# A hybrid decoder layer whose down projection puts tokens, not model columns, on the output partitions

## The chip, the cores and the metric

The kernel runs on one core of a Trainium2 chip. The metric is the device time of one execution in microseconds (us), the median of several runs. Engines are named as in the profile: PE is TensorE's matmul, PEld its weight load, DVE is VectorE, ACT ScalarE, POOL GpSimd, SP the engine that issues most DMAs.

## The reference

One layer for 512 prompt tokens and for 32 sample tokens (8 sequences of 4 new tokens, each with a past of 4096 rows in a paged cache). All data are f32; model width 1024, feed-forward width 4096.

```
h   = x + W_out [ DiffAttn(4 heads) ; ChunkGatingMLP(512 channels) ](RMSNorm(x))
out = h + W_down relu(W_up RMSNorm(h))^2
```

The feed-forward part is the one that the change concerns:

```python
def sq_relu_ffn(h, g, w_up, w_down):
    return jnp.square(jax.nn.relu(rms_norm(h, g) @ w_up)) @ w_down
```

The row scale r of RMSNorm is left out of the activations in the kernel: relu(r z)^2 = r^2 relu(z)^2, so the down projection's result is multiplied by r^2, token by token, and then added to h.

## The kernel before, in words

**Precision.** A product in f32 is made of three matmuls on fp32r halves: high by high, high by low, low by high. Weights come as raw f32 pieces of 512 KB (four blocks of 128 rows by 256 columns); `w_conv` (line 262) splits a piece into `wh` (cast on ACT) and `wl` (subtraction on DVE); `w_get` (line 280) hands the pair to PE. `w_issue` (line 241) starts loads on SP in the order of the list `WL`, at most `RAWB` ahead.

**Stages.** Up to some 363 us: input projection, prompt attention, gating, output projection (`out_proj`, line 1051), with tokens on the output partitions; a matmul there has 128 tokens stationary and 256 weight columns moving. The residual rows h stand in `hN[t]`, token tile t on the partitions. `h_tr` (line 1126) transposes h into eight tiles `acc[m]`, model columns on the partitions; `h_split` (line 1133) writes the halves `Thi` and `Tlo`. Then come eight groups of 512 feed-forward channels (`ffn`, line 1140). The decode attention (`micro`) is fed in between by `pump` (line 691): each `yield` of the main work gives a cost, and steps of the attention are emitted in proportion. It ends in group 4.

**A group.** Up: for each of four blocks of 128 channels, 24 matmuls with weights stationary and tokens moving. `square` (nested in `ffn`) does relu on ACT, the square on DVE, the high half `ahi` on ACT and the low half `alo` on DVE. Down: four blocks of 256 model columns (`dp`), weights stationary, tokens moving, result in accumulator tiles with model columns on the partitions; DVE adds them to `acc[m]`. In the first three activation slices both halves of 128 columns are begun before the fourth slice is touched.

**Sample tokens.** In groups 0 to 4 moving columns are the 512 prompt tokens. The sample's h is ready only in group 4 (`out_sample`, line 1315). Groups 5 to 7 (joint) move 544 columns, in two matmuls of 272. The sample's share of groups 0 to 4 is made up for by `ffn_sample` (line 1248) inside groups 5 to 7, from unsplit f32 weights: `tiled` (line 1243) puts four products of 32 tokens side by side on the PE array, which leave four partial sums on the 128 partitions of `ysum`.

**Row scale and end.** The sum in `acc` starts as h divided by r^2: `spread` (line 1107) brings the factors of the tokens to all partitions with four products with `ones`, and multiplies `acc`. In the last group `sum_sample` (line 1273) joins the four partial sums, and `finish` (line 1223), put off by `later` until the next `flush` (line 295), transposes a block of columns back (two transposes for the sample, eight for the prompt), scales by r^2 and stores.

**Order.** Instructions are emitted in the order of the code, and a planner then fixes each engine's order from modelled times. `Ordered` (line 41) limits it: on PE and DVE an instruction may go at most 28 places ahead.

Of the kernel before, what the change touches and what calls it, by code (L numbers as in the profile page):

```python
# [30 lines left out]
NPL = 6  # L31
PLX = 2
WINDOW = 28
P_AT = 10
# [28 lines left out]
def kernel(  # L63
# [53 lines left out]
    def second_phase():  # L117
        local.close()
        phase1.close()
        pools["tw"] = T  # L120
        local_pool(8)
        pools["w"] = ctx.enter_context(tc.tile_pool(name="wp2", bufs=2))
        psd2 = ctx.enter_context(tc.tile_pool(name="psd2", bufs=3, space=bass.MemoryType.PSUM))
        pools["ps"] = [psd, psd2, psd, psd2, psd, psd2, psd, psd]
        st["plain"] = NPL
        while w_issue():
            pass
        for _ in range(2):
            w_conv()
# [32 lines left out]
    alo = []  # L162
    ysum = []
    idt = const.tile([128, 128], F32, name="idt")
    ones = const.tile([128, 128], F32, name="ones")
# [59 lines left out]

    def add(main, extra=(), rate=1):
        for n, pieces in enumerate(main):
            WL.extend((w, True) for w in pieces)
            WL.extend((w, False) for e in extra for x in e[rate * n:rate * n + rate] for w in x)

    add(wo_pieces())
    for g in range(NG):
        add(group_pieces(g), [wo_pieces()] if g == G1 - 1 else [group_pieces(j) for j in samples(g)] if g >= G1 else (),
            2 if g == NG - 1 else 1)

    raws = []
    plain = []
    cvt = []
    st = {"next": 0, "issued": 0, "done": 0, "plain": 0}

    def w_issue(t=None):

        if st["next"] == len(WL):
            return False
        src, split_it = WL[st["next"]]
        if split_it:
            if t is None:
                if st["issued"] >= st["done"] + RAWB:
                    return False
                t = wp.tile([128, 4, 256], F32, tag="raw", name="raw", bufs=RAWB)  # L250
            raws.append(t)
            st["issued"] += 1
        else:
            if len(plain) >= st["plain"]:
                return False
            t = pools["w"].tile([128, 4, 256], F32, tag="plain", name="plain", bufs=st["plain"] + PLX)
            plain.append(t)
        SP.dma_start(out=t, in_=src)
        st["next"] += 1
        return True  # L260

    def w_conv():

        i = st["done"]
        if raws:
# [8 lines left out]
            V.tensor_tensor(out=lo, in0=raw, in1=hi, op=ALU.subtract)  # L274
            cvt.append((hi, lo))
            st["done"] += 1
            while w_issue():
                pass

    def w_get():  # L280
        return cvt.pop(0)

# [8 lines left out]
    def later(fn, d=1):  # L291

        pend[d - 1].append(fn)
# [757 lines left out]
    def out_proj(att):  # L1051
        acc.extend(R[2 + m // 4][:, (m % 4) * T:(m % 4) * T + T] for m in range(8))
        ss = ssb[0]
        for p in range(4):
            A_, B_ = w_get(), w_get()
            cols = slice(256 * p, 256 * p + 256)
            for tp in range(2):
# [6 lines left out]
                if p == 3 and tp == 1:  # L1064
                    for m in range(6):
                        h_split(m, slice(0, 256), acc[m][:, 0:256])
                if p == 2 and tp == 0:
                    for t in (R[2], R[3]):
                        G.memset(t.rearrange("p (m t) -> p m t", m=4)[:, :, 512:544], 0.0)
                for half, w in W:  # L1070
# [33 lines left out]
        V.tensor_scalar(out=ms, in0=ms, scalar1=EPS, scalar2=None, op0=ALU.add)  # L1104
        V.tensor_copy(out=rst8, in_=ms)

        def spread():
            psr = dt_()
            for t in range(4):
                dg = zt_()[:, 0:128]  # L1110
                V.tensor_scalar(out=dg, in0=idt, scalar1=rst8[:, t:t + 1], scalar2=None, op0=ALU.mult)
                mm(psr[:, 128 * t:128 * t + 128], ones, dg, True, True)
            rb = tt_()
            A.copy(out=rb[:, 0:512], in_=psr)
            for m in range(8):
                V.tensor_tensor(out=acc[m][:, 0:512], in0=acc[m][:, 0:512], in1=rb[:, 0:512], op=ALU.mult)
            rsqrt(ms, 0.0)
            V.tensor_tensor(out=rst[:, 0:4], in0=ms, in1=ms, op=ALU.mult)
        later(spread)
        for i in range(2):  # L1120
            t = big.tile([128, 4 * T], F32R, tag=f"r{i}", name=f"a{i}")
            for o in (0, 2 * T):
                ahi.append(t[:, o:o + T])
                alo.append(t[:, o + T:o + 2 * T])
# [15 lines left out]
    def ffn(start, joint, last, small):  # L1140
        rng = [(0, 272), (272, 544)] if joint else [(0, 512)]
        n = T if joint else TP

        def step():
# [4 lines left out]
        def square(ps, ff):  # L1149
            r = tt_()  # L1150
            for q, (a, e) in enumerate(rng):
                A.activation(out=r[:, a:e], in_=ps[q][:, 0:e - a], func=ACTF.Relu)
            V.tensor_tensor(out=r[:, 0:n], in0=r[:, 0:n], in1=r[:, 0:n], op=ALU.mult)
            A.copy(out=ahi[ff][:, 0:n], in_=r[:, 0:n])
            V.tensor_tensor(out=alo[ff][:, 0:n], in0=r[:, 0:n], in1=ahi[ff][:, 0:n], op=ALU.subtract)

        for pr in range(2):
# [17 lines left out]
            for f in range(2):  # L1175
# [19 lines left out]
                yield 2.8  # L1195
            step()
        for dp in range(4):
            hiw, low = w_get()
            ps = [[dt_() for _ in rng] for _ in range(2)]
            for ffs in ((0, 1), (2, 3)) if last else ((0, 1, 2), (3,)):  # L1200
                if ffs[0]:
                    flush()
                for d in range(2):
                    dc = slice(128 * d, 128 * d + 128)
                    for ff in ffs:
                        for w, (st_w, mv) in enumerate(((hiw, ahi), (hiw, alo), (low, ahi))):
                            for q, (a, e) in enumerate(rng):
                                mm(ps[d][q][:, 0:e - a], st_w[:, ff, dc], mv[ff][:, a:e], ff == 0 and w == 0, ff == 3 and w == 2)
            w_conv()
            for d in range(2):  # L1210
                m = 2 * dp + d
                for q, (a, e) in enumerate(rng):
                    V.tensor_tensor(out=acc[m][:, a:e], in0=acc[m][:, a:e], in1=ps[d][q][:, 0:e - a], op=ALU.add)
            step()
            if last and dp == 0:
                later(sum_sample)
            yield 5.6
            if last:
                later(lambda dp=dp: finish(dp))
        if last:  # L1220
            flush()

    def finish(dp):

        cols = slice(256 * dp, 256 * dp + 256)
        ps = dt_()
        for d in range(2):
            PE.transpose(ps[0:32, 128 * d:128 * d + 128], acc[2 * dp + d][:, 512:544], idt)
        zs = zt_()
        V.scalar_tensor_tensor(out=zs[0:32], in0=ps[0:32, 0:256], scalar=rst[0:32, 4:5], in1=ysum[0][0:32, cols],  # L1230
                               op0=ALU.mult, op1=ALU.add)
        SP.dma_start(out=ys[:, cols], in_=zs[0:32])
        for tp in range(2):
            ps = dt_()
            for k in range(4):
                t, d = 2 * tp + k // 2, k % 2
                PE.transpose(ps[:, 128 * k:128 * k + 128], acc[2 * dp + d][:, 128 * t:128 * t + 128], idt)
            z = tt_()[:, 0:512]
            V.tensor_scalar(out=z[:, 0:256], in0=ps[:, 0:256], scalar1=rst[:, 2 * tp:2 * tp + 1], scalar2=None, op0=ALU.mult)
            A.activation(out=z[:, 256:512], in_=ps[:, 256:512], func=ACTF.Copy, scale=rst[:, 2 * tp + 1:2 * tp + 2])  # L1240
            SP.dma_start(out=yp[:, 2 * tp:2 * tp + 2, cols], in_=z.rearrange("p (t c) -> p t c", t=2))

# [5 lines left out]
    def ffn_sample():  # L1248
# [17 lines left out]
        for dp in range(4):  # L1266
# [4 lines left out]
            yield 0.5  # L1271

    def sum_sample():
        t = pools["w"].tile([32, 1024], F32, tag="xs", name="part", bufs=1)
        for b in range(1, 4):
            A.copy(out=t, in_=ysum[0][32 * b:32 * b + 32, :])
            V.tensor_tensor(out=ysum[0][0:32], in0=ysum[0][0:32], in1=t, op=ALU.add)
        V.tensor_scalar(out=ysum[0][0:32], in0=ysum[0][0:32], scalar1=rst[0:32, 4:5], scalar2=None, op0=ALU.mult)

# [35 lines left out]
    def out_sample():  # L1315
        stack.append(pools["w"].tile([128, 32], F32, tag="stack", name="stack", bufs=1))
        for b in range(4):
            V.tensor_copy(out=stack[0][32 * b:32 * b + 32], in_=idt[32 * b:32 * b + 32, 32 * b:32 * b + 32])
        xs = pools["w"].tile([32, 1024], F32, tag="xs", name="hs", bufs=1)
        SP.dma_start(out=xs, in_=xs_d)  # L1320
        for p in range(4):
# [21 lines left out]
        def go():  # L1343
# [11 lines left out]
            G.memset(y, 0.0)  # L1355
            V.tensor_scalar(out=y[0:32], in0=xs, scalar1=ss[:, 0:1], scalar2=None, op0=ALU.mult)
            rsqrt(ss[:, 0:1], 0.0)
            V.tensor_tensor(out=rst[0:32, 4:5], in0=ss[:, 0:1], in1=ss[:, 0:1], op=ALU.mult)
        later(go)
# [44 lines left out]
```

## Time and profile before

| | us |
|---|---|
| timed runs, median (lowest, highest) | 843.15 (841.08, 843.17) |
| profiled execution, its own time | 842.67 |
| its span | 841.0 |
| PE busy in the span | 812.3 (97%) |
| PEld, DVE, ACT, POOL busy | 630.6, 547.7, 357.9, 187.0 |

Busy is the time in which at least one instruction of the engine runs. Matmuls overlap one another, so that PE's share tells that it seldom stands still, and not how fast it goes; the distance between two starts tells that.

### The profile page before, as it was taken

The numbers are of one execution on the slowest core, as the hardware profiler recorded it, in microseconds if no ns is written. First come the engines' busy times: TensorE is split into PE (matmuls) and PEld (weight loads), VectorE is DVE, ScalarE is ACT, GpSimd is POOL, SyncE is SP. The second block draws the span as 40 slices with busy tenths as digits, with TensorE's granted clock in tenths as the row PEclk, the third lists the DMA queues.
The fourth block names the chain that finished last, engine by engine and source line by source line (L and its number), as shares of the span: only waits on it lengthen the run. The fifth ranks groups of instructions, "written<-read, shape, count | busy, mean of one in ns | idle before, by whom it ended". The sixth has DMA issues, their size and how long they took to land.

```text
span 841.0 us, 15425 instructions
## 1 busy us (share of the span) xinstructions
PE 812.3 (97%) x6210; PEld 630.6 (75%) x6210; DVE 547.7 (65%) x957; ACT 357.9 (43%) x888; POOL 187.0 (22%) x196
## 2 busy tenths in 40 slices
PE   5899999999899999999999999999999999999997
PEld 5788788676566788876666766655776898998997
DVE  5978766899888954787767576633844535444354
ACT  4543734776564652735144144163332431331231
POOL 4453532243432321212222232120100000000000
PEclk8899999999999999999999999999999999999999
DMA  8496799788788889877989797786398177577302
GB/s 316 156 376 227 264 356 317 298 317 328 279 312 322 296 307 334 291 244 281 321 316 344 294 346 275 281 294 230 116 317 267 61 237 245 177 234 232 101 14 94
DMA packets 101796, 219.06 MB, mean 260 GB/s; under 512 B 6088, under 2 KB 83996, under 8 KB 85340
## 3 DMA queue, kind: packets, MB, share of 16 engines
q0 software_dynamic: 18432, 134.23, 42.7%
q1 hardware_dynamic: 83292, 83.84, 30.5%
q8 instruction: 49, 0.80, 0.4%
q14 instruction: 23, 0.19, 0.1%
HBM read 213.53 MB, written 4.52 MB: 259 GB/s over the span
## 4 chain that ended last, share of the span: by engine, by line
PE 77%; DVE 8%; ACT 7%; DMA 5%; issue 2%; POOL 1%; SPq 0%; DVEq 0%; POOLq 0%; ACTq 0%
PE d L52 66%; PE O L52 6%; PE S L52 5%; DVE kt L52 3%; ACT PT L52 3%; DMA kraw<-in_cache_k_dram,idxK 2%; DMA raw<-in_w_in_dram 2%; DVE wl L52 1%; ACT wh L52 1%; DMA sg<-in_subln_gain_dram 1%; ACT z L52 1%; DVE s L52 1%; ACT t L52 1%; DVE zn L52 1%; ACT P L52 0%
## 5 line engine op out<-in xcount | busy, mean ns | idle before, releaser
L52 ACT CAST wh<-raw 128x1024 fp32r<-128x1024 f32 x90 | 94.1, 1047 | 189.2 <-PE d L52 175.4
L52 PE MATMUL d<-a,wh 128*128 128x272 f32 (+1 forms) x704 | 168.2, 342 | 0.4 <-DVE a L52 0.4
L52 DVE STREAM_TRANSPOSE kt<-kraw 128x2048 f32<-128x2048 f32 x64 | 146.8, 2300 | 13.5 <-PE S L52 7.1
L52 DVE TENSOR_TENSOR wl<-raw,wh 128x1024 fp32r<-128x1024 f32 x90 | 109.3, 1218 | 54.6 <-ACT wh L52 54.2
L52 PEld LDWEIGHTS d<-a,wh 128*128 128x128 f32 x704 | 112.8, 188 | 29.4 <-issue 7.1
L52 POOL DMA_INDIRECT v<-in_cache_v_dram,idxK x64 | 72.9, 1139 | 269.8 <-PE O L52 252.2
L52 PE MATMUL d<-wh,Thi 128*128 128x256 f32 x432 | 127.6, 296 | 0.6 <-ACT d L52 0.5
L52 PE MATMUL d<-wl,Thi 128*128 128x256 f32 x432 | 122.4, 283 | 0.0
L52 PE MATMUL d<-wh,Tlo 128*128 128x256 f32 x432 | 122.1, 283 | 0.2 <-DVE Tlo L52 0.2
L52 PE MATMUL d<-Thi,wh 128*128 128x272 f32 (+2 forms) x368 | 109.8, 339 | 0.0
L52 PE MATMUL d<-Tlo,wh 128*128 128x272 f32 (+2 forms) x368 | 106.7, 330 | 1.9 <-DVE Tlo L52 1.9
L52 PE MATMUL d<-Thi,wl 128*128 128x272 f32 (+2 forms) x368 | 106.8, 330 | 0.0
L52 PE MATMUL d<-a,wl 128*128 128x272 f32 (+1 forms) x352 | 102.7, 336 | 0.0
L52 PEld LDWEIGHTS d<-wh,Thi 128*128 128x128 f32 x432 | 81.6, 189 | 17.1 <-issue 11.5
L52 POOL DMA_INDIRECT kraw<-in_cache_k_dram,idxK x64 | 69.1, 1080 | 104.5 <-DVE kt L52 59.8
L52 PEld LDWEIGHTS d<-wh,Tlo 128*128 128x128 f32 x432 | 81.6, 189 | 0.9 <-issue 0.4
L52 PEld LDWEIGHTS d<-Thi,wh 128*128 128x128 f32 x368 | 63.7, 189 | 24.5 <-issue 15.0
L52 PEld LDWEIGHTS d<-wl,Thi 128*128 128x128 f32 x432 | 81.4, 188 | 0.0
L52 PE MATMUL O<-v,PT 128*32 128x512 f32 x512 | 73.4, 607 | 1.2 <-ACT PT L52 1.2
L52 ACT COPY PT<-d 32x128 f32<-32x128 f32 x256 | 65.6, 256 | 14.4 <-DVE d L52 11.0
L52 PEld LDWEIGHTS d<-Tlo,wh 128*128 128x128 f32 x368 | 63.9, 189 | 8.5 <-DVE Tlo L52 2.2
L52 PEld LDWEIGHTS d<-Thi,wl 128*128 128x128 f32 x368 | 63.7, 189 | 6.1
(265 smaller groups left out, 1069.3 us busy)
## 6 DMA issues: line engine op xcount, KB each, us to landing
raw<-in_w_up_dram SPq DMA_DIRECT2D x32, 512.0 KB, 5.3
raw<-in_w_down_dram SPq DMA_DIRECT2D x32, 512.0 KB, 3.9
plain<-in_w_up_dram SPq DMA_DIRECT2D x20, 512.0 KB, 4.3
plain<-in_w_down_dram SPq DMA_DIRECT2D x20, 512.0 KB, 6.0
raw<-in_w_in_dram SPq DMA_DIRECT2D x18, 512.0 KB, 8.2
raw<-in_w_out_dram SPq DMA_DIRECT2D x8, 512.0 KB, 6.6
plain<-in_w_out_dram SPq DMA_DIRECT2D x8, 512.0 KB, 8.7
r<-in_x_prompt_dram SPq DMA_DIRECT2D x4, 512.0 KB, 8.3
```

The lines of the kernel that those rows point to most:

```text
L52: r = f(*args, **kw)
```

## The change

The down projection turns round. The activations are stationary (128 tokens), 256 weight columns move, and the result has tokens on the partitions, where DVE scales it by r^2 and adds it to `hN[t]` in one instruction (`total`). `acc` is no longer a sum; `spread`, the accumulator adds, `finish` and its transposes go, and in the last group `total` issues the store. Two token tiles share one accumulator bank of 512 columns; block 0 takes a third bank, since there the fourth activation slice comes last for three token tiles. In the joint groups the sample tokens leave the down matmuls: their activations are kept unsplit in `apk`, the raw down weights are kept in four tiles (`KEEP`), and `sample_down` multiplies them by column tiles, two blocks at a time, into `ysum`. `sample_out` joins the four partial sums with a product with `stack` and stores. The scratch pool shrinks by four tiles, the descriptor space of the software DMA from its default to 8192 bytes, and the cost 5.6 of a column block is given to `pump` as twice 2.8. The put-off work (`flush`) comes ahead of a block's matmuls, in block 0 behind the first 27.

```diff
@@ -30,6 +30,7 @@
...
 PLX = 2
+KEEP = 4
@@ -118,7 +119,7 @@
...
         pools["tw"] = T
-        local_pool(8)
+        local_pool(4)
@@ -161,6 +162,7 @@
...
     ysum = []
+    xsh = []
@@ -223,19 +225,20 @@
...
 
-    def add(main, extra=(), rate=1):
+    def add(main, extra=(), rate=1, keep=False):
         for n, pieces in enumerate(main):
-            WL.extend((w, True) for w in pieces)
+            WL.extend((w, 2 if keep and n >= 2 else True) for w in pieces)
...
         add(group_pieces(g), [wo_pieces()] if g == G1 - 1 else [group_pieces(j) for j in samples(g)] if g >= G1 else (),
-            2 if g == NG - 1 else 1)
+            2 if g == NG - 1 else 1, g >= G1)
...
     cvt = []
+    kept = []
@@ -247,7 +250,8 @@
...
                     return False
-                t = wp.tile([128, 4, 256], F32, tag="raw", name="raw", bufs=RAWB)
+                t = (pools["w"].tile([128, 4, 256], F32, tag="keep", name="keep", bufs=KEEP) if split_it == 2 else
+                     wp.tile([128, 4, 256], F32, tag="raw", name="raw", bufs=RAWB))
@@ -273,11 +277,13 @@
...
             cvt.append((hi, lo))
+            kept.append(raw)
...
     def w_get():
+        kept.pop(0)
@@ -1064,9 +1070,6 @@
...
                         h_split(m, slice(0, 256), acc[m][:, 0:256])
-                if p == 2 and tp == 0:
-                    for t in (R[2], R[3]):
-                        G.memset(t.rearrange("p (m t) -> p m t", m=4)[:, :, 512:544], 0.0)
@@ -1102,23 +1105,9 @@
...
         V.tensor_scalar(out=ms, in0=ms, scalar1=EPS, scalar2=None, op0=ALU.add)
-        V.tensor_copy(out=rst8, in_=ms)
-
-        def spread():
-            psr = dt_()
-            for t in range(4):
-                dg = zt_()[:, 0:128]
-                V.tensor_scalar(out=dg, in0=idt, scalar1=rst8[:, t:t + 1], scalar2=None, op0=ALU.mult)
-                mm(psr[:, 128 * t:128 * t + 128], ones, dg, True, True)
-            rb = tt_()
-            A.copy(out=rb[:, 0:512], in_=psr)
-            for m in range(8):
-                V.tensor_tensor(out=acc[m][:, 0:512], in0=acc[m][:, 0:512], in1=rb[:, 0:512], op=ALU.mult)
-            rsqrt(ms, 0.0)
-            V.tensor_tensor(out=rst[:, 0:4], in0=ms, in1=ms, op=ALU.mult)
-        later(spread)
+        V.reciprocal(out=rst[:, 0:4], in_=ms)
         for i in range(2):
-            t = big.tile([128, 4 * T], F32R, tag=f"r{i}", name=f"a{i}")
+            t = big.tile([128, 4 * T], F32R, tag=f"r{2 + i}", name=f"a{i}")
@@ -1140,6 +1129,7 @@
...
         n = T if joint else TP
+        apk = pools["w"].tile([128, 4, 32], F32, tag="apk", name="apk", bufs=4) if joint else None
@@ -1151,8 +1141,10 @@
...
             V.tensor_tensor(out=r[:, 0:n], in0=r[:, 0:n], in1=r[:, 0:n], op=ALU.mult)
-            A.copy(out=ahi[ff][:, 0:n], in_=r[:, 0:n])
-            V.tensor_tensor(out=alo[ff][:, 0:n], in0=r[:, 0:n], in1=ahi[ff][:, 0:n], op=ALU.subtract)
+            A.copy(out=ahi[ff][:, 0:TP], in_=r[:, 0:TP])
+            V.tensor_tensor(out=alo[ff][:, 0:TP], in0=r[:, 0:TP], in1=ahi[ff][:, 0:TP], op=ALU.subtract)
+            if joint:
+                A.copy(out=apk[:, ff, :], in_=r[:, TP:T])
@@ -1194,51 +1186,68 @@
...
             step()
+        own = []
+
+        def sample_down():
+
+            for cols, raw in own:
+                ps = dt_()[:, 0:256]
+                tiled(ps, apk, raw, True, True)
+                V.tensor_tensor(out=ysum[0][:, cols], in0=ysum[0][:, cols], in1=ps, op=ALU.add)
+            del own[:]
+
         for dp in range(4):
+            cols = slice(256 * dp, 256 * dp + 256)
+            if joint and not (last and dp == 3):
+                own.append((cols, kept[0]))
             hiw, low = w_get()
-            ps = [[dt_() for _ in rng] for _ in range(2)]
-            for ffs in ((0, 1), (2, 3)) if last else ((0, 1, 2), (3,)):
-                if ffs[0]:
-                    flush()
-                for d in range(2):
-                    dc = slice(128 * d, 128 * d + 128)
-                    for ff in ffs:
-                        for w, (st_w, mv) in enumerate(((hiw, ahi), (hiw, alo), (low, ahi))):
-                            for q, (a, e) in enumerate(rng):
-                                mm(ps[d][q][:, 0:e - a], st_w[:, ff, dc], mv[ff][:, a:e], ff == 0 and w == 0, ff == 3 and w == 2)
+            ps = [dt_() for _ in range(3 if dp == 0 else 2)]
+            at = [ps[0][:, 0:256], ps[-1 if dp == 0 else 0][:, 0 if dp == 0 else 256:][:, 0:256], ps[1][:, 0:256],
+                  ps[1][:, 256:512]]
+
+            def down(t, ffs):
+                tok = slice(128 * t, 128 * t + 128)
+                for ff in ffs:
+                    for w, (st_a, mv) in enumerate(((ahi, hiw), (ahi, low), (alo, hiw))):
+                        mm(at[t], st_a[ff][:, tok], mv[:, ff, :], ff == 0 and w == 0, ff == 3 and w == 2)
+
+            def total(t):
+                V.scalar_tensor_tensor(out=hN[t][:, cols], in0=at[t], scalar=rst[:, t:t + 1], in1=hN[t][:, cols],
+                                       op0=ALU.mult, op1=ALU.add)
+                if last:
+                    SP.dma_start(out=yp[:, t, cols], in_=hN[t][:, cols])
+
+            if dp == 0:
+                for t in range(3):
+                    down(t, (0, 1, 2))
+            flush()
+            for t in range(4):
+                down(t, (3,) if dp == 0 and t < 3 else range(4))
+                total(t)
+                if t == 1:
+                    yield 2.8
             w_conv()
-            for d in range(2):
-                m = 2 * dp + d
-                for q, (a, e) in enumerate(rng):
-                    V.tensor_tensor(out=acc[m][:, a:e], in0=acc[m][:, a:e], in1=ps[d][q][:, 0:e - a], op=ALU.add)
+            if joint and dp % 2 == 1:
+                sample_down()
+            if last and dp == 2:
+                own.append((slice(768, 1024), kept[0]))
+                sample_down()
             step()
-            if last and dp == 0:
-                later(sum_sample)
-            yield 5.6
-            if last:
-                later(lambda dp=dp: finish(dp))
+            if last and dp == 2:
+                for k in range(2):
+                    sample_out(k)
+            yield 2.8
...
 
-    def finish(dp):
-
-        cols = slice(256 * dp, 256 * dp + 256)
-        ps = dt_()
-        for d in range(2):
-            PE.transpose(ps[0:32, 128 * d:128 * d + 128], acc[2 * dp + d][:, 512:544], idt)
-        zs = zt_()
-        V.scalar_tensor_tensor(out=zs[0:32], in0=ps[0:32, 0:256], scalar=rst[0:32, 4:5], in1=ysum[0][0:32, cols],
-                               op0=ALU.mult, op1=ALU.add)
-        SP.dma_start(out=ys[:, cols], in_=zs[0:32])
-        for tp in range(2):
-            ps = dt_()
-            for k in range(4):
-                t, d = 2 * tp + k // 2, k % 2
-                PE.transpose(ps[:, 128 * k:128 * k + 128], acc[2 * dp + d][:, 128 * t:128 * t + 128], idt)
-            z = tt_()[:, 0:512]
-            V.tensor_scalar(out=z[:, 0:256], in0=ps[:, 0:256], scalar1=rst[:, 2 * tp:2 * tp + 1], scalar2=None, op0=ALU.mult)
-            A.activation(out=z[:, 256:512], in_=ps[:, 256:512], func=ACTF.Copy, scale=rst[:, 2 * tp + 1:2 * tp + 2])
-            SP.dma_start(out=yp[:, 2 * tp:2 * tp + 2, cols], in_=z.rearrange("p (t c) -> p t c", t=2))
+    def sample_out(k):
+
+        cols = slice(512 * k, 512 * k + 512)
+        ps = dt_()[0:32, :]
+        mm(ps, stack[0], ysum[0][:, cols], True, True)
+        V.scalar_tensor_tensor(out=xsh[0][:, cols], in0=ps, scalar=rst[0:32, 4:5], in1=xsh[0][:, cols], op0=ALU.mult,
+                               op1=ALU.add)
+        SP.dma_start(out=ys[:, cols], in_=xsh[0][:, cols])
@@ -1269,13 +1278,6 @@
...
             yield 0.5
-
-    def sum_sample():
-        t = pools["w"].tile([32, 1024], F32, tag="xs", name="part", bufs=1)
-        for b in range(1, 4):
-            A.copy(out=t, in_=ysum[0][32 * b:32 * b + 32, :])
-            V.tensor_tensor(out=ysum[0][0:32], in0=ysum[0][0:32], in1=t, op=ALU.add)
-        V.tensor_scalar(out=ysum[0][0:32], in0=ysum[0][0:32], scalar1=rst[0:32, 4:5], scalar2=None, op0=ALU.mult)
@@ -1317,6 +1319,7 @@
...
         xs = pools["w"].tile([32, 1024], F32, tag="xs", name="hs", bufs=1)
+        xsh.append(xs)
@@ -1353,9 +1356,7 @@
...
             G.memset(y, 0.0)
-            V.tensor_scalar(out=y[0:32], in0=xs, scalar1=ss[:, 0:1], scalar2=None, op0=ALU.mult)
-            rsqrt(ss[:, 0:1], 0.0)
-            V.tensor_tensor(out=rst[0:32, 4:5], in0=ss[:, 0:1], in1=ss[:, 0:1], op=ALU.mult)
+            V.reciprocal(out=rst[0:32, 4:5], in_=ss[:, 0:1])
@@ -1388,7 +1389,8 @@
...
 
-    nc = _bacc.Bacc("TRN2", target_bir_lowering=False, num_devices=1)
+    nc = _bacc.Bacc("TRN2", target_bir_lowering=False, num_devices=1,
+                     dynamic_dma_scratch_size=8192)
```

## Rows read from the trace of the kernel before

**Rows 1.** One stretch: length, busy PE, PEld, DVE, ACT, POOL (instructions), PE clock, DMA, GB/s.

```profile
363.30:834.80 471.50, 469.91 (x3245) 361.10 (x3246) 263.24 (x399) 157.02 (x322) 57.34 (x54) 1.00 0.67 233
```

**Rows 2.** Who PE waited for from 363 us: us in total, times, longest.

```profile
PE d L52 <- DVE Tlo L52: 1.9, 1, 1.9
PE O L52 <- ACT PT L52: 1.2, 1, 1.2
PE d L52 <- DVE a L52: 0.4, 2, 0.2
```

**Rows 3.** Timeline of PE in a down projection: start us, duration us, instruction.

```profile
641.12 0.40 PE L52 MATMUL d<-a,wl 128*128 128x512 f32 x1
...
642.51 0.40 PE L52 MATMUL d<-a,wl 128*128 128x512 f32 x1
```

**Rows 4.** Timeline of PE in the output projection.

```profile
338.21 0.28 PE L52 MATMUL d<-wh,Thi 128*128 128x256 f32 x1
...
341.07 0.28 PE L52 MATMUL d<-wh,Thi 128*128 128x256 f32 x1
```

**Rows 5.** Timeline of PE in the down projection of group 5.

```profile
703.01 0.41 PE L52 MATMUL d<-a,wl 128*128 128x272 f32 x2
703.35 1.07 PE L52 MATMUL d<-plain,apk 128*32 128x256 f32 x16
704.35 0.77 PE L52 MATMUL d<-a,wh 128*128 128x272 f32 x4
...
704.96 0.41 PE L52 MATMUL d<-a,wl 128*128 128x272 f32 x2
...
707.23 0.41 PE L52 MATMUL d<-a,wl 128*128 128x272 f32 x2
```

**Rows 6.** Timeline of PE at a product of the decode attention.

```profile
439.45 1.07 PE L52 MATMUL d<-om,selb 128*64 128x512 f32 x2
440.36 0.23 PE L52 MATMUL d<-lm,selb 128*64 128x8 f32 x2
```

**Rows 7.** Timeline of PE at the transposes of a column block.

```profile
816.32 1.25 PE L52 MATMUL d<-idt,r 128*32 128x128 f32 x10
817.33 0.75 PE L52 MATMUL d<-a,wh 128*128 128x272 f32 x4
```

**Rows 8.** Timeline of PE at the spread of the row scale.

```profile
368.30 1.05 PE L52 MATMUL d<-z,ones 128*128 128x128 f32 x8
369.11 0.37 PE L52 MATMUL d<-Thi,wl 128*128 128x256 f32 x1
```

**Rows 9.** Timeline of all engines at the end.

```profile
834.43 0.41 PE L52 MATMUL d<-a,wl 128*128 128x272 f32 x2
...
836.29 0.46 DVE L52 SCALAR_TENSOR_TENSOR z<-d,cst,ysum 32x256 f32<-32x256 f32 x1
...
837.21 0.89 SPq L52 DMA_DIRECT2D out_dram<-t  x2
```

**Rows 10.** Timeline of ACT and DVE, fourth activation slice of group 1.

```profile
452.97 0.60 ACT L52 ACTIVATE t<-d 128x512 f32<-128x512 f32 x1
...
455.73 0.68 DVE L52 TENSOR_TENSOR t<-t 128x512 f32<-128x512 f32 x1
...
457.10 0.69 DVE L52 TENSOR_TENSOR a<-t,a 128x512 fp32r<-128x512 f32 x1 [0.69 <-ACT a L52]
```

**Rows 11.** Timeline of DVE and ACT at the scaling of one bank.

```profile
817.18 0.48 DVE L52 TENSOR_SCALAR t<-d,cst 128x256 f32<-128x256 f32 x1 [1.04 <-PE d L52]
...
817.70 0.47 ACT L52 ACTIVATE t<-d,cst 128x256 f32<-128x256 f32 x1 [0.48 <-DVE t L52]
```

**Rows 12.** Groups of PE by form, 834.86 to 835.2 us, then 835.2 to 835.6 us.

```profile
L52 PE MATMUL d<-idt,mix 128*128 128x128 f32 x2 | 0.4, 272 | 0.0
L52 PE MATMUL d<-idt,mix 128*32 128x128 f32 x1 | 0.3, 270 | 0.0
...
L52 PE MATMUL d<-idt,mix 128*128 128x128 f32 x3 | 0.5, 291 | 0.1
```

## The prediction

> **What bounds the kernel now.** I read the table of stretches first. Between 363.3 and 834.8 us TensorE (PE) is busy for 469.91 of 471.50 us at a granted clock of 1.00, the upper of its two levels (2.4 GHz) [rows 1]. The eight feed-forward groups lie there. Second, the list of waits: in these 478 us PE waits four times, 3.5 us in all: 1.9 us for a split on VectorE (DVE), 1.2 us for a copy of the decode attention and twice 0.2 us for the low half of an activation [rows 2]. The change touches nothing ahead of 363 us, so the time follows PE's own work in the groups, plus whatever waits are added. The third view is PE's timeline. A matmul's listed duration is of no use, since matmuls overlap; I take the distance between starts.
>
> **The change part by part.** The profiled execution has 842.67 us for a span of 841.0 us, 0.06% under the median 843.15 of the timed runs; the sum is made against 842.67.
>
> Prices of a down matmul, start to start. With 512 moving columns, 6 of them take 642.51 - 641.12 = 1.39 us, so 231.7 ns [rows 3]. With 256, 24 take 341.07 - 338.21 = 2.86 us, so 119.2 ns; these are the output projection's, which already has tokens stationary and weights moving, the very form that the down projection gets [rows 4]. With 272, 18 take 707.23 - 704.96 = 2.27 us, so 126.1 ns [rows 5].
>
> (a) Groups 0 to 4: 96 matmuls of 512 columns become 192 of 256. 192 x 0.1192 - 96 x 0.2317 = 22.89 - 22.24 = +0.65 us a group, five groups: +3.2 us. Twice the weight loads are issued; the 119.2 ns have them in, one load to each matmul.
>
> By the Trainium skill, page "TensorE: Matmul & The Clock Gate", section "Back-to-back issue gap", a warm matmul takes its columns over 2.4 GHz plus 2.5 ns, so halving it would cost 2.6 ns a pair, +1.2 us here as an estimate; the rows give 6.7 ns a pair, and I keep them.
>
> (b) Groups 5 to 7: 192 matmuls of 272 become 192 of 256, since the 32 sample tokens leave: 192 x 6.9 ns = 1.3 us, three groups: -4.0 us.
>
> (c) The sample tokens' own down product comes as column tiles: twelve calls of four f32 matmuls, in six visits of two calls. Two such calls stand in the trace: the matmul pair ahead starts at 703.01, so it would have been over for the next at 703.26, and that next one starts at 704.35: 1.09 us [rows 5]. Six visits: +6.5 us.
>
> (d) The partial sums of the sample are joined by two f32 matmuls of 512 columns. One of that width takes 440.36 - 439.45 = 0.91 us, with some 0.1 us of switch ahead [rows 6]: +2.0 us. The copies and adds on ScalarE (ACT) and DVE that it replaces lay beside PE work and give nothing.
>
> (e) The ten transposes behind each of the first three column blocks of the last group go: 817.33 - 816.32 = 1.01 us each [rows 7], -3.0 us.
>
> (f) The four f32 products that spread the row scale go: 369.11 - 368.30 = -0.8 us [rows 8]. The eight DVE products behind them lay under busy PE.
>
> (g) The end. Today the last matmul ends at 834.43 + 0.41 = 834.84, and accumulator adds, transposes, scalings and two stores follow; the last issue ends at 837.21 + 0.89 = 838.10, the span 2.9 us later: 6.2 us behind the last matmul [rows 9]. After, one DVE step of 256 columns follows, the 0.46 us of the z row there, and an issue of 0.45 us: 0.05 + 0.46 + 0.05 + 0.45 + 2.9 = 3.9 us. That is -2.3 us, but the last token tile itself waits for the sum of the one before (below) with nothing left to fill, +0.7 us: -1.6 us.
>
> Sum of (a) to (g): 3.2 - 4.0 + 6.5 + 2.0 - 3.0 - 0.8 - 1.6 = +2.3 us.
>
> (h) The fourth activation slice. Ahead of its products PE has today 18 matmuls of 512, 4.2 us; the new order has 27 of 256, 3.2 us. In group 1 the chain of that slice starts with the relu at 452.97, about when the down matmuls start, and ends with the low half at 457.10 + 0.69 = 457.79, 4.8 us later, its high half 4.1 us later [rows 10]. That cost the 0.2 us wait; with 1 us less cover it costs about 1.2 us, and groups 0 and 2, where conversions and key transposes also lie ahead on DVE, are alike. In the later groups DVE is freer. Bounds 0 (other matmuls are put ahead) and 3.7 us; I take +1.5, nearer the middle, since the order on PE can be planned around it (rows 12, below).
>
> (i) A new wait. Two token tiles now share one accumulator bank, and DVE's sum of the first must read that bank before the second is begun. That halves of a bank are kept apart shows at the end: DVE scales the left half of a bank from 817.18 to 817.66 and ACT, which takes the right half, starts at 817.70, released by DVE [rows 11]. Column block 0 has one such wait (it has a third bank), blocks 1 to 3 two: 7 a group, 56 in all. Left open, one costs the matmul's own 0.28 us less its 0.12 us slot, 0.46 us of DVE and 0.1 us of hand-over, some 0.7 us; all 56: 41 us. Behind the waiting matmul on PE stands everything, but the planner can put other matmuls first: the code names the two transposes of 32 columns first, yet at the end of the kernel one of these and two of 128 columns go ahead of the wait for the adds [rows 12], and the other of 32 comes later. The third token tile lies in another bank and offers twelve matmuls, 1.4 us, against 0.7 us. What stays is where DVE is later than planned. The nearest row is rows 12's own wait, with its fill: 0.1 us of idle. I take under half of that, 0.04 us, since only the first groups have a crowded DVE: 56 x 0.04 = +2.2 us. Bounds 0 and 41.
>
> The hand-over of the sample's helpers now comes ahead of a block's matmuls instead of amid them; in group 4 two small products would find their copy (0.4 us) just begun. Bounds 0 to 1.2 us; the same fill hides it, 0. Four held weight tiles, smaller scratch pools, sixteen narrower stores: PE waits for no weight transfer and no store behind 363 us [rows 2], so 0; if the smaller descriptor space held the gathers of keys back, up to the 1.2 us of rows 2 once more.
>
> Forecast: 2.3 + 1.5 + 2.2 = +6.0 us, 842.67 + 6.0 = **848.7 us**.
>
> **The rivals.**
> 1. Everything new is hidden by planned order: +2.3 us, 845.0. For it: only four waits behind 363 us [rows 2], over hundreds of hand-overs. Against it: two of these four are the very chain of (h).
> 2. DVE's queue decides. In groups 0 to 2 key transposes and weight conversions stand in order ahead of the sums. In rows 10 the relu is over at 453.57 and its square starts on DVE at 455.73, 2.2 us late; if a sum is late by that, the spare of the fill (1.4 - 0.7 us) leaves 1.5 us, and if 9 of the 21 waits there meet it, 13 us, with (h) in full 3.7 and the 2.3: +19, 862. For it: those rows. Against it: DVE's wait for PE before the accumulator adds means that it is often free.
> 3. The shared bank in strict order, unfilled: 41 + 3.7 + 2.3 = +47, 890. Against it: rows 12. The Trainium skill, page "PSUM — Partial Sum Buffer", section "PSUM bank collisions raise a hardware error", asks that engines be kept apart by bank, not by address; by that rule the waits are there, and the trace agrees (the 0.04 us between DVE's end and ACT's start).
> 4. Not slower. Group 0 loses eight DVE products and the sums come in finer pieces, so the four old waits of 3.5 us close, while all new ones are filled: 2.3 - 3.5 = -1.2 us, 841.5. It decides from the point where DVE runs ahead of PE throughout groups 0 to 3. Against it: the largest of the four ends at 363.2, ahead of any removed product. To be faster by 0.3% the rates of (a) or (c) would have to be lower as well.
>
> **How the numbers follow.** Forecast 0.45 (its own range 845.7 to 853), rival 1 0.23, rival 2 0.14, rival 3 0.04, rival 4 0.14. About 0.3%, 2.5 us, is what a measurement of this kernel can tell from no change, so 840.6 to 845.7 is "same". Faster takes the lower half of rival 4: 0.08. Same takes the rest of it and most of rival 1: 0.27. Slower: 0.65. The range takes in rival 4's centre and rival 2's: 841.5 to 862.
>
> **What would show it.** (a), (b): the 256-column form of a-stationary matmuls at 119 ns between starts, groups 0 to 4 longer by 0.65 us, 5 to 7 shorter by 1.3 us before the column tiles. (c), (d): six visits of 1.1 us and two f32 products of 512 columns. (e) to (g): some 3.9 us from last matmul to end. (h), (i): PE's waits on DVE's activation halves and on hN in the list of waits, 4 us together. Wrong if the form runs at another rate, if PE's waits on hN pass 10 us, or if PE's order shows no other matmul between the two tiles of a bank.

## The result and the profile after

The changed kernel takes **861.85 us** (median of 4, 860.5 to 862.58) against 842.12 (840.25 to 843.17) for the kernel before: a ratio of **1.0235 [1.0209, 1.026]**, 19.7 us slower. The forecast was 6 us slower, 848.7: the direction was right, the size was not. The profiled execution took 861.99 us, its span 860.3.

The page of after, three groups of part 5 (busy us, mean ns of one | idle before, releaser):

```profile
L53 PE MATMUL d<-wh,a 128*128 128x256 f32 x1024 | 201.2, 290 | 1.8 <-DVE a L53 1.2
...
L53 PE MATMUL d<-wl,a 128*128 128x256 f32 x512 | 144.7, 283 | 0.0
...
L53 DVE SCALAR_TENSOR_TENSOR h<-d,cst,h 128x256 f32<-128x256 f32 x128 | 59.6, 479 | 78.7 <-PE d L53 78.0
```

The new form is there, 1536 matmuls, and DVE's 128 sums `h` stood idle 78 us waiting for PE: DVE was not what was late. Then the stretch that answers to [rows 1] and who PE waited for, as in [rows 2]:

```profile
363.30:856.90 493.60, 488.69 (x3785) 388.73 (x3783) 268.55 (x426) 151.18 (x324) 53.08 (x52) 0.99 0.65 223
```
```profile
PE d L53 <- DVE Tlo L53: 1.9, 1, 1.9
PE d L53 <- ACT zn L53: 1.2, 2, 0.9
PE d L53 <- DVE a L53: 1.2, 1, 1.2
PE O L53 <- ACT PT L53: 1.2, 1, 1.2
PE d L53 <- DVE t L53: 0.6, 1, 0.6
PE d L53 <- DVE h L53: 0.6, 1, 0.6
```

The stretch is 22 us longer, and 18.8 us of that is *busy* time: 488.69 against 469.91. The waits come to 6.7 us where [rows 2] had 3.5. Of the 56 new waits on `h` the list has one left, the last (0.6 us). So the planner filled them, as forecast, and yet the time is lost. It is inside PE's own work, and there the start-to-start distances have to be added up by kind of matmul, since listed durations overlap. This table, worked out from PE's records behind the 2 us wait on `Tlo`, is the ledger the rest goes by (us; "runs" are unbroken series of one kind; broken sets are explained behind the table; e1 and e9 are experiments below):

```
                               before   after   e1_pair  e9_wideall
down products                  190.81   199.56   191.10   184.37
  in so many stretches             36       58       36       35
column-tiled f32 products       75.39    90.79    81.18    80.33
  decode attention O, S         52.06    56.48    51.94    51.54
  sample, plain tiles           23.33    27.98    23.80    23.24
  sample, kept tiles (new)          -     6.33     5.44     5.55
  in so many runs                  62      100       74       70
  broken sets of four               0       41        6        3
join of partial sums (new)          -     1.89     1.81     1.81
transposes, row-scale spread     5.12        -        -        -
up products, all forms         188.14   187.67   186.67   187.25
other small products            13.27    13.77    13.72    13.55
all                            472.73   493.68   474.48   467.31
```

Against before, the down products took 8.7 us more, and column-tiled products that the change does not touch (decode attention's S and O, the plain tiles) 9.1 us more. Those have the same instructions; they stand in 91 runs for 62. What that does is seen in group 5 (PE's timeline, start, duration, instruction):

```profile
709.40 0.28 PE L53 MATMUL d<-wh,a 128*128 128x256 f32 x1
709.61 1.05 PE L53 MATMUL d<-plain,apk 128*32 128x256 f32 x10
710.60 0.38 PE L53 MATMUL d<-wh,a 128*128 128x256 f32 x1
710.82 0.28 PE L53 MATMUL d<-wl,a 128*128 128x256 f32 x1
710.93 0.40 PE L53 MATMUL d<-wh,a 128*128 128x256 f32 x2
...
712.01 0.28 PE L53 MATMUL d<-wh,a 128*128 128x256 f32 x1
712.22 0.63 PE L53 MATMUL d<-plain,apk 128*32 128x256 f32 x6
712.78 0.38 PE L53 MATMUL d<-wh,a 128*128 128x256 f32 x1
```

Sixteen column-tiled matmuls that stood in one run of 1.00 us [rows 5] are cut in 10 and 6: 710.60 - 709.61 = 0.99 us and 712.78 - 712.22 = 0.56 us, 1.55 for 1.00. On the other side the last matmul ahead of a run takes 0.21 us and the first behind it 0.22 (710.82 - 710.60) where the pace is 0.12: two more such edges, another 0.2 us.

PE's single records, which the timeline merges, show what the cut breaks. Four products side by side start within 0.014 us of one another, and the next four about 0.20 us later (0.42 where 512 columns move, as in O). The run of 16 is four such sets; the 10 and 6 are six: 4, 4, 1, 1 and 3, 3. A set broken in one and three takes the time of two. In the kernel before all sets are whole, after 41 are broken. The twelve matmuls between the 10 and the 6 are exactly the fill that the prediction counted as free.

### The profile page after: what moved, and what is told of

Same layout as the page of the kernel before. It is cut to its first block, busy times and chain, and to the rows that moved or that the text cites. A ratio compares the mean times of both kernels' runs of the same rounds, so it can differ in the third digit from the quotient of the medians.

```text
span 860.3 us, 16516 instructions
## 1 busy us (share of the span) xinstructions
PE 830.2 (97%) x6742; PEld 658.2 (77%) x6742; DVE 550.8 (64%) x981; ACT 351.2 (41%) x888; POOL 181.3 (21%) x192
## 3 DMA queue, kind: packets, MB, share of 16 engines
q0 software_dynamic: 18432, 134.23, 41.9%
## 5 line engine op out<-in xcount | busy, mean ns | idle before, releaser
L53 PE MATMUL d<-wh,a 128*128 128x256 f32 x1024 | 201.2, 290 | 1.8 <-DVE a L53 1.2
L53 PEld LDWEIGHTS d<-wh,a 128*128 128x128 f32 x1024 | 163.7, 190 | 28.5 <-issue 13.3
L53 ACT CAST wh<-raw 128x1024 fp32r<-128x1024 f32 x78 | 81.5, 1047 | 205.3 <-PE d L53 177.4
L53 PE MATMUL d<-wl,a 128*128 128x256 f32 x512 | 144.7, 283 | 0.0
L53 DVE TENSOR_TENSOR wl<-raw,wh 128x1024 fp32r<-128x1024 f32 x78 | 95.0, 1219 | 55.5 <-ACT wh L53 52.3
L53 DVE SCALAR_TENSOR_TENSOR h<-d,cst,h 128x256 f32<-128x256 f32 x128 | 59.6, 479 | 78.7 <-PE d L53 78.0
L53 PEld LDWEIGHTS d<-wl,a 128*128 128x128 f32 x512 | 97.4, 190 | 0.1
L53 POOL DMA_INDIRECT kraw<-in_cache_k_dram,idxK x64 | 66.8, 1044 | 101.9 <-DVE kt L53 54.9
L53 PE MATMUL O<-v,PT 128*32 128x512 f32 x512 | 77.0, 606 | 1.2 <-ACT PT L53 1.2
```

What stands on the lines that cost most here:

```text
L53: r = f(*args, **kw)
```

## The experiments

Two theories stood at the start. **A, the fill costs**: the order that the planner chooses to avoid waiting on the shared bank cuts runs, and each cut has a price. **B, the queue or the helpers**: late sums on DVE, or the sample's put-off helper work that now comes ahead of a block, make PE late.

**e1_pair**: the two sums of a bank are issued together, behind both of its token tiles.

```
-                total(t)
+                if t % 2 == 1:
+                    total(t - 1)
+                    total(t)
```

> The changed kernel, but the two sums of a bank come together behind both token tiles, so that TensorE never waits in the middle of a bank. Theory A (the shared bank makes the planner cut up runs of column-tiled matmuls, and every cut costs 0.2 to 0.6 us): the 9.1 us that the kept column-tiled groups cost more and some 3 us of switches go, so 12 us less than the changed kernel: 850 us (847 to 853). Theory B (the halved matmuls and the finer feeding of the decode attention cost it, whatever the bank): within 3 us of the changed kernel, 859 to 863.

844.14 us (842.56 to 846.5), ratio 1.0042 [1.0022, 1.0061], a larger gain than theory A's 12 us. Its waits from 362 us:

```profile
PE d L53 <- DVE Tlo L53: 2.0, 1, 2.0
PE d L53 <- DVE a L53: 1.4, 2, 1.2
PE O L53 <- ACT PT L53: 1.2, 1, 1.2
PE d L53 <- ACT zn L53: 0.5, 1, 0.5
```

And the sample's tiles in one run again:

```profile
697.51 0.28 PE L53 MATMUL d<-wh,a 128*128 128x256 f32 x1
697.72 1.07 PE L53 MATMUL d<-plain,apk 128*32 128x256 f32 x16
698.72 0.39 PE L53 MATMUL d<-wh,a 128*128 128x256 f32 x1
```

17.7 us less than the changed kernel by the medians, 16.5 when each is set against the kernel before on its own chip (840.92 here): most of the 19.7 is gone with the order of the sums alone, no instruction added or removed. In the ledger there are 26 runs and 22 stretches fewer; the tiled products fall by 9.6 us (0.37 a run) and the down products by 8.5. Of the 41 broken sets 35 are whole again: 28 at 0.20 us and 7 of O at 0.42 make 8.5 of the 9.6. Theory A holds for the bulk.

**e2_strict**: as the changed kernel, with PE held to program order in the down projection.

```
+        PE.window = 1
         for dp in range(4):
...
+        PE.window = WINDOW
```

> The changed kernel with TensorE held to the order of the code inside the down projection, so that nothing is put into the wait for a sum. Theory A: 56 waits stand open at 0.7 us, some 41 us, against 12 us of cuts that go: 885 us or more (range 875 to 900). Theory B: the waits are short or absent anyway, within 5 us of the changed kernel.

906.75 us, ratio 1.077 [1.0728, 1.0812], above the expected range:

```profile
PE d L53 <- DVE h L53: 41.9, 52, 2.3
```

This is rival 3's world. The listed waits are 41.9 us, but the down products took 254.23 us, 63.1 more than in e1: 1.2 us for each of 52 waits against the 0.7 that I had priced; some 5 us of the 63.1 are the lower clock, as told under the rivals below. The planner's fill saves over two thirds of that, and is still 17.7 us dearer than not having the waits.

**e12_strictpair**: both edits, pairs of sums and strict order.

> Sums by pairs with TensorE held to the order of the code in the down projection. Theory A: the 45 us of the strict run with the shared bank were the 56 open waits alone, so here the strict order costs next to nothing: 844 to 846. If a strict order costs by itself (the decode attention's products can't move ahead): 850 or more.

844.61 us, ratio 1.0034 [1.0016, 1.0052], the same as e1. Strict order as such costs nothing; it was dear in e2 for the wait alone.

**e5_bank**: single sums as in the change, but a bank of its own for each token tile.

```
-            ps = [dt_() for _ in range(3 if dp == 0 else 2)]
-            at = [ps[0][:, 0:256], ...
+            at = [dt_()[:, 0:256] for _ in range(4)]
```

> The changed kernel, but each of the four token tiles has a bank of its own in every column block; sums, put-off work and feeding stay where the change has them. Theory A (the shared bank alone): the same gain as with the sums by pairs, about 844 us (842 to 848), column-tiled runs whole again. Theory B' (not the bank but the later, paired sums on VectorE made the gain): within 3 us of the changed kernel, 859 to 863.

843.08 us, ratio 1.0015 [0.9998, 1.0032]. Another cure for the same cause: what cost some 17 us is two tiles sharing a bank with a reader between them. The Trainium skill, page "PSUM — Partial Sum Buffer", section "PSUM bank collisions raise a hardware error", asks that accesses of two engines to one bank be guarded by semaphores, by bank and not by address. These kernels do so; with a bank for each tile PE's list has no wait on `h` (a new one of 1.6 us is for a gather of `v`), and e2 shows what the guard costs where two tiles share one.

**e10_cut**: e1 with nine more cuts made by hand: in the groups with sample tokens each of the two sample calls of an odd block is set among the last token tile's matmuls.

```
                 for ff in ffs:
+                    if joint and dp % 2 == 1 and t == 3 and own and ff % 2 == 1:
+                        sample_down(1)
```

> Sums by pairs, no wait added, but the column-tiled calls of the sample tokens in groups 5 to 7 are put by hand among the matmuls of the last token tile of a block instead of behind them, which makes nine more stretches of down matmuls (45 for 36). Theory A: a cut costs about 0.3 us by itself, so 2.7 us more than sums by pairs, at unchanged waits of TensorE. If a cut is free and only the waits cost, as sums by pairs.

847.64 us, ratio 1.0076 [1.0051, 1.0101]; on the same chip e12 took 844.61, 3.0 us less. Its list of waits is e1's, entry for entry. In its ledger 45 stretches of down products for 36 take 192.92 us (+1.8), and the kept tiles, ten of eleven runs cut to 8, 6.58 (+1.1): a third of a microsecond a cut, with no wait in play:

```profile
704.47 0.28 PE L53 MATMUL d<-wh,a 128*128 128x256 f32 x1
704.68 0.64 PE L53 MATMUL d<-keep,apk 128*32 128x256 f32 x8
705.25 0.39 PE L53 MATMUL d<-wh,a 128*128 128x256 f32 x1
```

These cuts fall between sets of four and break none (6 broken, as in e1): a piece of 8 takes 0.57 us, two of them 1.14 for 1.00 in one run, and the edges of the down products add 0.2. The cuts that the planner makes in the changed kernel break sets and cost more for that. The 3.0 us are not much over what two such timings resolve, and O (+0.9) and the up products (+0.6) rose as well in this profile, for no reason that I can see.

**e3_flush**, **e4_pairflush**: theory B's part. The helpers' work goes back to the middle of blocks 1 to 3, without and with e1's pairs.

```
             for t in range(4):
+                if dp > 0 and t == 2:
+                    flush()
```

> The changed kernel with the put-off work of column blocks 1 to 3 emitted in the middle of the block's matmuls, as before, instead of ahead of them. If the place of this work costs what the trace shows (two waits for a copy on ScalarE 1.2 us, one for DVE 0.6 us with sparse transposes, and 3.4 us at half clock behind it, 1.5 us): 3 to 5 us less, 857 to 859 us. If the planner only moves these waits elsewhere: within 1 us of the changed kernel.

> Both edits, sums by pairs and put-off work in the middle. If the two costs are separate, they add: 15 to 17 us less than the changed kernel, 845 to 847 us; that is the sum of the counted terms of the prediction (+2.3 us) plus one or two us of the fourth activation slice. If they are one cost (the sparse transposes only appear since the order is cut up), as e1_pair.

e3 took 860.79 us (1.0243 [1.02, 1.0287]), no gain where some was expected; e4 848.57 (1.0088 [1.0062, 1.0113]), 4.4 us *worse* than e1. The waits on `zn` went, as B said, and a longer one on `t` came, 1.8 and 2.4 us. Behind it stands the clock. The stretches of e4 (length; busy PE, PEld, DVE, ACT, POOL; clock; DMA share; GB/s):

```profile
600.00:603.40 3.40, 1.11 (x10) 0.91 (x8) 2.36 (x5) 0.85 (x2) 1.22 (x2) 1.00 0.30 81
603.40:610.20 6.80, 6.64 (x29) 5.75 (x30) 2.62 (x9) 0.53 (x2) 0.99 (x1) 0.50 0.40 134
610.20:620.00 9.80, 9.80 (x69) 9.11 (x69) 6.13 (x9) 3.05 (x3) 0.00 (x0) 1.00 0.86 285
```

After 3.4 us with PE busy for only 1.11 the granted clock fell to the lower level (1.2 GHz) for 6.8 us. The changed kernel has a smaller one at the same place:

```profile
607.00:610.00 3.00, 2.38 (x16) 1.66 (x15) 2.00 (x6) 0.27 (x1) 0.16 (x1) 1.00 0.38 109
610.00:614.00 4.00, 4.00 (x21) 3.97 (x21) 1.92 (x5) 0.84 (x2) 0.99 (x1) 0.57 0.81 271
```

where 16 down matmuls took 213 ns for 119, 1.5 us. There PE follows four short DVE steps, one 32-column transpose at a time:

```profile
607.06 0.28 PE L53 MATMUL d<-wh,a 128*128 128x256 f32 x1
607.96 0.21 PE L53 MATMUL d<-idt,t 32*128 32x32 f32 x1 [0.62 <-DVE t L53]
```

**e8_cadence**: e4 with one hand-over to the helpers a block (`yield 5.6` at its end) in place of two of 2.8, so that none stands right ahead of the put-off work.

> Sums by pairs, put-off work in the middle of blocks 1 to 3, and one yield of 5.6 at the end of a block as in the kernel before, instead of two of 2.8. If the loss of the run with put-off work in the middle (2.4 us of waiting for VectorE and 6.8 us at half clock behind it) came from a yield right ahead of the put-off work, it is gone: about 844 us, no stretch at half clock after 370 us. If the place of the put-off work alone made it, 848.

844.43 us, ratio 1.0036 [1.0021, 1.005]: the wait on `t` and the low clock are gone, and it stands level with e1. So e4's loss was this hand-over, and the helpers' place is worth nothing beyond it.

**e7_nosample**: e1 without the sample tokens' own down product (`sample_down` does nothing; those rows of the output lack it).

> Sums by pairs, with the column-tiled down product of the sample tokens in groups 5 to 7 left out (these tokens lack three eighths of their feed-forward part). The prediction's term (c) says 6.5 us, the trace of sums by pairs 5.4 us plus switches: 838 us (837 to 839.5). If the column tiles lie in time that TensorE loses anyway, 843 to 844.

836.66 us, ratio 0.9937 [0.9918, 0.9955]. Against e1's 1.0042 that is 1.05%, some 8.8 us, give or take 2. By e1's ledger the tiles are 5.44 us, and the whole ledgers of e1 and e7 differ by 5.2 us (474.48 and 469.27): four of the six runs stand next to a run of plain tiles, which has the edges anyway. Term (c), 6.5, lies between the two; why the timed runs give more than the profiled ones is not shown (e1's profiled execution was the fastest of its ten, e7's the slowest of its four).

**e6_wide**, **e11_mix**, **e9_wideall**: can the halved matmuls of (a) be avoided? The down weights of a group are read as two blocks of 512 columns, by halves of the hidden channels, and each token tile has a bank: in groups 4 to 7 (e6, the others as e1; e11, the others as e5), or in all groups (e9).

```
+            down = [[wd[:, 4 * g + 2 * fh:4 * g + 2 * fh + 2, 512 * c:512 * c + 512]] for c in range(2) for fh in range(2)]
...
+            at = [dt_() for _ in range(4)]
```

> Sums by pairs, and in groups 4 to 7 the down weights come as pieces of two channel blocks by 512 columns, so that a matmul moves 512 columns into a bank that one token tile has alone. From the row prices (231.7 ns for 512, 119.2 for 256): a group's down projection is 0.65 us shorter than in 256-column form, four groups: 2.6 us less than sums by pairs, about 841.5 us, near the kernel before; 840 to 843. If the halving of the matmuls costs nothing in a stream, as with sums by pairs, 844.

> A bank for each token tile everywhere, 512 columns in groups 4 to 7, 256 in groups 0 to 3. Own banks were 1 us better than sums by pairs, so 1 us under the wide run with pairs: 839 to 840. If that 1 us was noise: 840 to 841.

> All eight groups with 512 moving columns and a bank for each token tile. From the row prices the down projection of groups 0 to 3 is another 2.6 us shorter than with wide groups 4 to 7 alone (840.7): 838 to 839, 0.3% under the kernel before. Against it: groups 0 to 3 have five banks, four of them now open at once, and the decode attention needs two for some steps; if TensorE waits for them, 841 to 846 and waits in the list that the other runs have not.

e6: 840.68 us, ratio 0.9988 [0.9975, 1.0002], as expected. e11: 842.69, 1.0013 [0.9998, 1.0028], above what was expected; its profiled span, 838.2, would have fitted, the timed median does not, and I can't say why. e9: **837.84 us, ratio 0.9949 [0.993, 0.9967]**, 0.5% faster than the kernel before. Its down products take 184.37 us, 6.7 less than e1's, in half the instructions. Of the 6.7, 1.4 are e1's waits on `a`, which are gone; the rest is about 7 ns for each of 768 pairs, where (a) had 6.7. PE waits twice:

```profile
PE d L53 <- DVE Tlo L53: 2.0, 1, 2.0
PE O L53 <- ACT PT L53: 1.2, 1, 1.2
```

## Why the prediction was right in direction and wrong in size

**Terms (a) to (g)**, +2.3 together, hold. e1, which has all of them but the last wait of (g), and no wait on a bank, is 0.42%, 3.5 us, over the kernel before, where 2.3 and 1.5 for (h) make 3.8. One by one: the pace of the form was 119 ns, as read from the output projection; down products +0.3 in e1 where (a) and (b) say -0.8, and 1.0 of the difference is the longer wait on `a` of (h), which the ledger has among them; the kept tiles 5.44 by the ledger, 8.8 by e7's time, for (c) 6.5; the join 1.81 for (d) 2.0; transposes and spread -5.1, of which (e) and (f) say -3.8 and the rest belongs to the end. For (g) the last wait and the tail:

```profile
855.21 0.39 PE L53 MATMUL d<-wh,a 128*128 128x256 f32 x1 [0.58 <-DVE h L53]
...
856.62 0.28 PE L53 MATMUL d<-wh,a 128*128 128x256 f32 x1
856.95 0.48 DVE L53 SCALAR_TENSOR_TENSOR h<-d,cst,h 128x256 f32<-128x256 f32 x1 [1.80 <-PE d L53]
```

That is 0.58 us for the 0.7, and 860.28 - 856.91 = 3.4 us from the last matmul to the end for the 3.9.

**Term (h)**, +1.5: the waits on `a` are 1.2 us after, 1.4 in e1, for 0.4 before. Right, rather high.

**Term (i) is the step that failed.** It said "56 x 0.04 = +2.2 us", the idle time left over where the planner fills. That idle time is there, 0.6 us in the list and 1.6 us in twelve places too short to be listed. There a matmul starts 0.05 to 0.06 us after a sum `h` has ended on DVE, and its start and that of the next are late by 0.13 us together. One of the twelve:

```profile
404.91 0.48 DVE L53 SCALAR_TENSOR_TENSOR h<-d,cst,h 128x256 f32<-128x256 f32 x1
405.31 0.53 PE L53 MATMUL d<-wh,a 128*128 128x256 f32 x2
405.68 0.28 PE L53 MATMUL d<-wl,a 128*128 128x256 f32 x1
```

The sum ends at 405.39, the second matmul of the pair starts 0.06 us later, and the pair takes 0.37 us to the next start for 0.24. But the fill was valued at nothing: "The third token tile lies in another bank and offers twelve matmuls, 1.4 us, against 0.7 us", as if those twelve would cost the same anywhere. They stand where a run of column-tiled matmuls had been, and the planner's own choice among what is ready also takes S, O and sample tiles as fill. By e1 all that went with the order of the sums was 17.7 us, 0.32 us for each of 56. In the ledgers of after and e1 (19.2 us apart) 9.6 lie in the tiled products (8.5 of it by the 35 broken sets, 0.4 a wait on `zn`) and 8.5 in the down products, of which about 1.3 are listed waits, 1.6 the twelve unlisted ones, 1.5 the low clock and the remaining 4 the edges of 22 more stretches; the last 1.0 is in the up products. So the fill itself, which the prediction had at 0, took some 13 us: 9 in the tiled products and 4 at the edges. None of the three signs of being wrong came (119 ns held, the waits on hN were 2.2 us in all and not 10, other matmuls stood between the tiles): they asked for the wait and not for the price of the fill.

**The helpers' hand-over**, put at 0 (bounds 0 to 1.2): 1.2 us on `zn`, the bound, and beyond it 0.6 us on `t` and 1.5 us of low clock, which I had not thought of. e1 has 0.5 of it.

**The rivals.** Rival 2 named 862 and the time is 861.85, but its mechanism is not there: DVE's sums wait for PE, not PE for them. The number agrees by accident. Rival 3's order was run (e2): 62.6 us over e1, so its 41 for the waits was too low. A wait lasted 0.8 us, not 0.46 + 0.1, and the first matmul behind it takes 0.22 us. Some 5 us more are the clock, which the rival had not: in four stretches between 541 and 649 us, where PE had stood in such waits, 56 down matmuls start 213 ns apart (granted clock 0.74 over 632.5 to 639 us, 1.2 GHz in about half of it). Rivals 1 and 4 fall for the changed kernel; with the sums paired (e1) rival 1's 845.0 is about what one gets.

Two slips of arithmetic change nothing: the 2.6 ns a pair behind (a) is 2.5, and 56 waits at the parts named in (i), 0.72 us, are 40.3 and not 41.

What cuts cost is settled in the main: e10's cost 0.3 to 0.4 us, those of the changed kernel some 0.5 with both sides counted, and the difference is the broken sets. What stays open is why e7's timed runs give more than its ledger, why e11's median is above e6's, and where the 1.0 us of the up products comes from.

## What to carry to other kernels

A reordering that fills a wait is not free: ask what order it breaks. Count, ahead of the change, the runs of each kind of matmul, and price a cut by the timeline: what the last and the first matmul of one kind lose at the edge, and what the cut run loses. Where products go side by side in sets, see to it that a set is never cut. Where two results share a bank and are read one at a time, read them together or give each a bank, before anything is planned around the wait; and a list of waits that stays short while the engine's busy time grows means that the loss is in the order.

## What the runs showed of the hardware

A change between full-width matmuls and column-tiled f32 ones costs on both sides: 0.21 us for the last and 0.22 for the first full-width matmul at a pace of 0.12, and 16 tiled ones take 1.00 us in one run, 1.14 in two runs of 8 (e10), 1.55 in runs of 10 and 6. The four products of a set start within 0.014 us of one another, sets of 256 columns 0.20 us apart, so that a set broken in one and three takes twice as long. A stretch in which PE had few matmuls among its waits (busy 1.11 of 3.4 us in e4, 2.38 of 3.0 us after) was followed by the lower clock level for 6.8 and some 3.4 us; in e1 and e8 the granted clock from 600 to 620 us, without the wait on `t`, stayed at 1.00.
